# One block kernel: a norm weight spread by products, last steps by banks, two matrices moved to VectorE, later attention turns

## The chip, the cores and the metric

The kernel runs on one core of a Trainium2 chip. The metric is device time in microseconds (us) of one execution; lower is better. The engines are named as in the profile: PE (TensorE products), PEld (TensorE weight loads), DVE (VectorE), ACT (ScalarE), POOL (GpSimd) and SP (the queue that issues nearly all transfers).

## The reference

The input is x of 256 rows by 1024 columns in float32. Two layers follow one another, each of three phases that add to x: a first feed-forward part, a mixer, a second feed-forward part.

```python
def _rms_norm(x, g):
    y = xf * lax.rsqrt(jnp.mean(xf * xf, axis=-1, keepdims=True) + NORM_EPS)
    return (y * g.astype(jnp.float32)).astype(x.dtype)

h = _rms_norm(x, ffn1_norm_pre[l])
x = x + 0.5 * _rms_norm(_swiglu(h, ffn1_w_gate[l], ffn1_w_up[l], ffn1_w_down[l]), ffn1_norm_post[l])
h = _rms_norm(x, mix_norm_pre[l])
x = x + _rms_norm(_mixer(h, w_in[l], ...), mix_norm_post[l])
h = _rms_norm(x, ffn2_norm_pre[l])
x = x + 0.5 * _rms_norm(_swiglu(h, ffn2_w_gate[l], ffn2_w_up[l], ffn2_w_down[l]), ffn2_norm_post[l])
```

The feed-forward width is 2816. The mixer multiplies h by w_in (8520 columns) and feeds three branches: sparse attention with a selected set of 64 keys (job `dsa`), a recurrence over 256 steps in eight heads of 64 (RWKV), and differential attention (job `diff`: two softmaxes, the second one subtracted with a factor lambda, then a norm of each head). Sigmoid gates weigh the three projected branches, their sum goes through w_out.

## The kernel before

Rows of x are held in two tiles of 128 tokens, called t = 0 and t = 1. Every weight is loaded in float32 (`raw`, at most 1 MB in one transfer, two buffers) and split into a rounded part `wh`, cast by ACT, and the rest `wl`, subtracted by DVE; both are of 128x1024. The activations are split in the same way (`hh`, `hl`), and one product becomes three: rest times `wh`, main times `wh`, main times `wl` (`mm3`, lines 229 to 235). Products of 512 columns are issued about 0.23 us apart.

`steps_b` makes a list of steps for one product of a tile: a step has a load and split (`ld`) and the products of one tile t (`go`). For the last product of a phase (w_down in 22 steps, w_out in 8) the output has 1024 columns, two PSUM banks of 512. `run_skew` puts the steps in order: the first `head` steps run for t = 0 and then for t = 1, the middle ones alternate t, and the last `tail` = 7 steps run for t = 0 and then for t = 1, so that tile 0 ends earlier than tile 1 and its norms have the time of tile 1's seven steps. Splits of these seven steps go to seven extra buffers.

`post_norm` (line 384) follows the last step of a tile: two squares with a sum on ACT (L330), the sum and epsilon on DVE (L332), the power of -1/2 on POOL (L333), then for each half a multiplication by the root and the weight from PSUM (L391) and one by the factor with the addition to x (L392). `pre_norm` (line 336) does the same for the norm ahead of the next phase (L330, L332, L333, L353), and its `rest` transposes the result on PE (L362) and splits it into `h`. The place of these transposes in PE's queue is set by `run_skew`: the deferred call is taken ahead of the last step of the other tile.

At the very start the weight of the first norm (`gpre`) is loaded as 128 copies of one row (512 KB). 13 products of zeros run on PE before the norm of tile 0, and 6 behind its transposes (`keep_warm`, L172).

In the mixer, attention and recurrence are generators (`dsa`, `diff`, and one that runs `rwkv_pre`, `rwkv_solve` and `rwkv`). After every step of the gate products, `tick` advances each job by one `yield`, so that their small products stand between the large ones in PE's queue. The order inside an engine is fixed when the program is built, and an engine works through it in order: the first instruction that waits holds up all behind it. In `rwkv_solve` the inverses of 16x16 blocks come back from DRAM as `zs` and `xs`; DVE spreads `zs` over four matrices `Z` (L1032), POOL spreads `xs` over two matrices `T` (L1036), and three levels of products with masks follow (`W`, L1063, and the update of `Z`, L1074). In `diff`, each pair of heads has scores `lm` (L767), a softmax (L653 to L656), two combining operations (L773, L774), then `LAG` = 2 yields, and the transposes of `lm` on PE (L196).

Of the kernel before, what the change touches and what calls it, by code (L numbers as in the profile page):

```python
# [22 lines left out]
WARM = 13, 6  # L23
# [16 lines left out]
class Block:  # L40
    def __init__(self, tc, ins, out, ctx):
# [21 lines left out]
        self.first = ()  # L63
# [39 lines left out]
    def constants(self):  # L103
# [8 lines left out]
        jf = jz[:, :128]  # L112
        with self.pn():
            nc.gpsimd.iota(jf, pattern=[[1, 128]], base=0, channel_multiplier=-1, allow_small_or_imprecise_dtypes=True)
# [98 lines left out]
    def split(self, src, k, n, pool=None):  # L213
# [3 lines left out]
        with self.p0(), self.behind(*(self.first if self.last is None else ())):  # L217
            pair = self.split_to(hi, lo, src)
        if self.last is None:
            self.first = pair  # L220
# [17 lines left out]
    def run_skew(self, steps, head=0, tail=0):  # L238

        n = len(steps)  # L240
        order = [(t, i) for t in range(2) for i in range(head)]
        order += [(t, i) for i in range(head, n - tail) for t in range(2)]
        order += [(t, i) for t in range(2) for i in range(n - tail, n)]
        held = {}
        for j, (t, i) in enumerate(order):
            if self.later and (head and j == head - 1 or tail and j == len(order) - 1):
                self.later.pop(0)()
            if t == 0:
                wait = RING <= i < head or i >= n - tail
                held[i] = steps[i][0](self.extra if wait else self.ring)  # L250
            steps[i][1](t, held[i])
            self.tick()

    def steps_b(self, rows, n, ksteps, xk, psum, done=None):
# [5 lines left out]
        def mk(k0):  # L260
# [7 lines left out]
            def go(t, w):  # L268
# [8 lines left out]
                if k0 + per == ksteps and done is not None:  # L277
# [45 lines left out]
    def rstd(self, parts, width):  # L323
# [8 lines left out]
        nc.vector.tensor_scalar(r, ss[:, 0:1], ss[:, 1:2], EPS, op0=OP.add, op1=OP.add)  # L332
# [3 lines left out]
    def pre_norm(self, t):  # L336
# [11 lines left out]
        with self.pn():  # L348
            xs = [self.x[t][:, h * 512:(h + 1) * 512] for h in range(2)]
            r = self.rstd(xs, D)  # L350
            for h in range(2):
                xn = self.junk.tile([128, 512], F32, name="xn")
                nc.vector.scalar_tensor_tensor(xn, xs[h], r, g[:, h * 512:(h + 1) * 512], op0=OP.mult, op1=OP.mult)  # L353
                xns.append(xn)

        def rest():

            with self.pn(), self.behind(self.last):
# [6 lines left out]
                if self.last is None:  # L365
                    self.first = pair
# [373 lines left out]
    def diff(self, st, vd):  # L740
# [10 lines left out]
        for t in range(2):  # L751
# [5 lines left out]
            for h2 in range(2):  # L757
# [17 lines left out]
                for _ in range(LAG):  # L775
# [24 lines left out]
            yts.append(yt)  # L800
        for _ in range(2 * LAG):
# [194 lines left out]
    def rwkv_solve(self, Ls, strip):  # L996
# [32 lines left out]
        for q in range(4):  # L1029
# [4 lines left out]
            if q < 2:  # L1034
# [234 lines left out]
```

## Time and profile before

| what | value |
|---|---|
| three runs of the kernel | 1435.26 us median (1435.07 to 1437.74) |
| the profiled execution | 1437.46 us, its span 1435.8 us |
| PE busy | 1399.8 us, 97% of the span |
| DVE busy | 1012.3 us, 71% |
| ACT busy | 713.2 us, 50% |
| POOL busy | 77.5 us, 5% |
| mean granted clock of PE | 0.996 |
| read from HBM | 241.80 MB |

The span runs from the first to the last instruction of the profiled execution; its own time is 1.66 us more. A row of the timeline has its start, its length, engine, line, operation, output and inputs, their shapes, and a count where neighbours are merged; in brackets stands how long the engine stood idle before it, and what ended the wait. PE's records overlap: a product of 512 columns is shown with 0.39 us although the next one starts 0.23 us later.

### The profile page before, as it was taken

The numbers are of one execution on the slowest core, as the hardware profiler recorded it, in microseconds if no ns is written. First come the engines' busy times: TensorE is split into PE (matmuls) and PEld (weight loads), VectorE is DVE, ScalarE is ACT, GpSimd is POOL, SyncE is SP. The second block draws the span as 40 slices with busy tenths as digits, with TensorE's granted clock in tenths as the row PEclk, the third lists the DMA queues.
The fourth block names the chain that finished last, engine by engine and source line by source line (L and its number), as shares of the span: only waits on it lengthen the run. The fifth ranks groups of instructions, "written<-read, shape, count | busy, mean of one in ns | idle before, by whom it ended". The sixth has DMA issues, their size and how long they took to land.

```text
span 1435.8 us, 20311 instructions
## 1 busy us (share of the span) xinstructions
PE 1399.8 (97%) x8077; PEld 1203.1 (84%) x8077; DVE 1012.3 (71%) x1496; ACT 713.2 (50%) x1090; POOL 77.5 (5%) x92
## 2 busy tenths in 40 slices
PE   8999999999899999999999999999999999999997
PEld 5888879999688878888888888799887888788886
DVE  5777564988666877776567764659977668768753
ACT  5444454656463554444454444555545635544442
POOL 1000010121100000000000000100300000000000
PEclk9999999999999999999999999999999999999999
DMA  6665665455332564665646656554443326555653
GB/s 220 189 192 194 216 223 186 122 175 152 102 118 89 184 211 148 194 200 200 225 147 189 192 201 237 174 180 147 147 136 101 135 86 226 173 175 178 215 182 114
DMA packets 176407, 246.91 MB, mean 172 GB/s; under 512 B 17908, under 2 KB 128440, under 8 KB 176312
## 3 DMA queue, kind: packets, MB, share of 16 engines
q1 hardware_dynamic: 176312, 245.62, 52.6%
q8 instruction: 63, 1.03, 0.3%
q14 instruction: 32, 0.26, 0.1%
HBM read 241.80 MB, written 3.80 MB: 171 GB/s over the span
## 4 chain that ended last, share of the span: by engine, by line
PE 79%; DVE 9%; DMA 6%; ACT 3%; issue 2%; POOL 0%; SPq 0%; DVEq 0%; POOLq 0%; ACTq 0%
PE ps L310 28%; PE ps L233 11%; PE ps L235 11%; PE ps L234 11%; PE ps L193 7%; DVE wl L224 4%; PE ps L229 3%; PE ps L230 3%; PE ps L231 3%; ACT wh L224 2%; DMA raw<-in_w_in_dram 1%; DMA raw<-in_w_out_dram 1%; PE ps L196 1%; DMA zs<-d 1%; DMA raw<-in_ffn_w_gate_dram 1%
## 5 line engine op out<-in xcount | busy, mean ns | idle before, releaser
L224 DVE TENSOR_TENSOR wl<-raw,wh 128x1024 fp32r<-128x1024 f32 x438 | 531.8, 1222 | 240.4 <-ACT wh L224 239.2
L224 ACT CAST wh<-raw 128x1024 fp32r<-128x1024 f32 x438 | 452.9, 1045 | 453.3 <-PE ps L310 183.4
L310 PE MATMUL ps<-h,wh 128*128 128x512 f32 x1152 | 392.5, 393 | 0.0
L310 PE MATMUL ps<-h,wl 128*128 128x256 f32 x1152 | 300.2, 281 | 0.0
L310 PEld LDWEIGHTS ps<-h,wh 128*128 128x128 f32 x1152 | 206.1, 188 | 37.1
L310 PEld LDWEIGHTS ps<-h,wl 128*128 128x128 f32 x1152 | 216.9, 188 | 12.4
L233 PE MATMUL ps<-wh,h 128*128 128x512 f32 x384 | 160.0, 417 | 2.2 <-DVE h L224 1.9
L229 PE MATMUL ps<-h,wh 128*128 128x256 f32 (+1 forms) x560 | 158.6, 283 | 0.0
L230 PE MATMUL ps<-h,wh 128*128 128x256 f32 (+1 forms) x560 | 156.8, 280 | 0.0
L235 PE MATMUL ps<-wl,h 128*128 128x512 f32 x384 | 153.1, 399 | 2.8 <-DVE wl L224 2.8
L231 PE MATMUL ps<-h,wl 128*128 128x256 f32 (+1 forms) x560 | 155.7, 278 | 0.0
L234 PE MATMUL ps<-wh,h 128*128 128x512 f32 x384 | 152.2, 396 | 0.0
L233 PE MATMUL ps<-wh,gl 128*128 128x512 f32 x352 | 137.3, 390 | 0.0
L235 PE MATMUL ps<-wl,gh 128*128 128x512 f32 x352 | 137.0, 389 | 0.0
L234 PE MATMUL ps<-wh,gh 128*128 128x512 f32 x352 | 136.9, 389 | 0.0
L229 PEld LDWEIGHTS ps<-h,wh 128*128 128x128 f32 (+1 forms) x560 | 104.8, 187 | 2.0 <-issue 1.3
L230 PEld LDWEIGHTS ps<-h,wh 128*128 128x128 f32 (+1 forms) x560 | 104.9, 187 | 0.3
L231 PEld LDWEIGHTS ps<-h,wl 128*128 128x128 f32 (+1 forms) x560 | 104.7, 187 | 0.1
L235 PEld LDWEIGHTS ps<-wl,h 128*128 128x128 f32 x384 | 72.7, 189 | 22.6 <-DVE wl L224 5.6
L233 PEld LDWEIGHTS ps<-wh,h 128*128 128x128 f32 x384 | 72.5, 189 | 20.2 <-issue 3.3
L234 PEld LDWEIGHTS ps<-wh,h 128*128 128x128 f32 x384 | 72.8, 190 | 13.4
L235 PEld LDWEIGHTS ps<-wl,gh 128*128 128x128 f32 x352 | 66.1, 188 | 13.9
(272 smaller groups left out, 1715.0 us busy)
## 6 DMA issues: line engine op xcount, KB each, us to landing
raw<-in_w_in_dram SPq DMA_DIRECT2D x66, 1024.0 KB, 5.1
raw<-in_ffn_w_up_dram SPq DMA_DIRECT2D x44, 1024.0 KB, 5.4
raw<-in_ffn_w_down_dram SPq DMA_DIRECT2D x44, 1024.0 KB, 4.9
raw<-in_ffn_w_gate_dram SPq DMA_DIRECT2D x43, 1024.0 KB, 5.4
raw<-in_w_branch_dram SPq DMA_DIRECT2D x12, 1024.0 KB, 4.9
raw<-in_w_out_dram SPq DMA_DIRECT2D x8, 1024.0 KB, 5.6
gpre<-in_ffn_norm_pre_dram SPq DMA_DIRECT2D x4, 512.0 KB, 5.2
gpost<-in_ffn_norm_post_dram SPq DMA_DIRECT2D x4, 512.0 KB, 6.3
```

What stands on the lines that cost most here:

```text
L193: self.small = self.nc.tensor.matmul(*a, **k)
L196: self.small = self.nc.tensor.transpose(*a, **k)
L224: return self.nc.scalar.copy(hi, src), self.nc.vector.tensor_sub(lo, src, hi.bitcast(F32))
L229: mm(ps, wh, xl, start=first, stop=False)
L230: mm(ps, wh, xh, start=False, stop=False)
L231: self.last = mm(ps, wl, xh, start=False, stop=last)
L233: mm(ps, xl, wh, start=first, stop=False)
L234: mm(ps, xh, wh, start=False, stop=False)
L235: self.last = mm(ps, xh, wl, start=False, stop=last)
L310: self.last = mm(*a, start=k == i == 0, stop=k == 7 and i == 1)
```

## The change

Five edits are made together. (1) The weight of the very first norm is loaded as one row (4 KB) and spread over 128 partitions by two float32 products with a column of ones, into two PSUM banks; the products of zeros become 6, then 4 behind the spreading, then 6; the first splits of weights are ordered anew against the norm. (2) The last seven steps of a phase run by tile and by bank: all seven for bank 0, then all seven for bank 1. (3) In the norms the sum with epsilon goes from DVE to POOL, and in `post_norm` the weight and the factor are multiplied first, the root is applied in the addition to x. (4) The two matrices `T` are made by DVE, behind the third and fourth `Z`. (5) `diff` yields four times in place of two between the softmax and its transposes, and once more at the end of each tile.

```diff
-WARM = 13, 6
+WARM = 6, 4, 6
...
-        order += [(t, i) for t in range(2) for i in range(n - tail, n)]
+        order += [(t, i, b) for t in range(2) for b in range(2) for i in range(n - tail, n)]
...
-            if self.later and (head and j == head - 1 or tail and j == len(order) - 1):
+            if self.later and (head and j == head - 1 or tail and j == len(order) - 2):
...
-                    for b in range(nb):
+                    for b in range(nb) if only is None else (only,):
...
-        nc.vector.tensor_scalar(r, ss[:, 0:1], ss[:, 1:2], EPS, op0=OP.add, op1=OP.add)
+        nc.gpsimd.tensor_scalar(r, ss[:, 0:1], ss[:, 1:2], EPS, op0=OP.add, op1=OP.add)
...
-            self.gpre = self.bcast(self.ins[f"{ph}_norm_pre"][l], D, self.gbp, "gb", "gpre")
+            row = self.ins[f"{ph}_norm_pre"][l]
+            if self.last is None:
+
+                g = self.gbp.tile([128, D], F32, name="grow", tag="gb")[0:1, :]
+                with self.p0():
+                    nc.sync.dma_start(g, bass.AP(tensor=row.tensor, offset=row.offset, ap=[[D, 1], [1, D]]))
+                self.gpre = [self.bank(self.acc) for _ in range(2)]
+                with self.pn():
+                    for h in range(2):
+                        self.tr = nc.tensor.matmul(self.gpre[h], self.ones, g[:, h * 512:h * 512 + 512],
+                                                   start=True, stop=True)
+                self.keep_warm(WARM[1])
...
+            ys = []
             for h in range(2):
+                y = self.junk.tile([128, 512], F32, name="xn")
+                nc.vector.scalar_tensor_tensor(y, ps[h], factor, g[:, h * 512:h * 512 + 512], op0=OP.mult, op1=OP.mult)
+                ys.append(y)
+            for h, y in enumerate(ys):
                 s = slice(h * 512, h * 512 + 512)
-                y = self.junk.tile([128, 512], F32, name="xn")
-                nc.vector.scalar_tensor_tensor(y, ps[h], r, g[:, s], op0=OP.mult, op1=OP.mult)
-                nc.vector.scalar_tensor_tensor(self.x[t][:, s], y, factor, self.x[t][:, s], op0=OP.mult, op1=OP.add)
+                nc.vector.scalar_tensor_tensor(self.x[t][:, s], y, r, self.x[t][:, s], op0=OP.mult, op1=OP.add)
...
-                for _ in range(LAG):
+                for _ in range(2 * LAG):
                     yield
...
             yts.append(yt)
+            yield
...
-            if q < 2:
+            if q > 1:
                 Ts.append(self.ep.tile([128, 4, 128], F32, name="T", tag="s"))
-                nc.gpsimd.tensor_tensor(Ts[q].rearrange("p v (g x) -> p v g x", x=16),
-                                        xs[:, 4 * q:4 * q + 4, None, :].to_broadcast([128, 4, 8, 16]), even, op=OP.mult)
+                nc.vector.tensor_tensor(Ts[-1].rearrange("p v (g x) -> p v g x", x=16),
+                                        xs[:, 4 * q - 8:4 * q - 4, None, :].to_broadcast([128, 4, 8, 16]), even, op=OP.mult)
```

VectorE's queue in the first mixer, from the arrival of `zs` on, before (`blk` is the mask of 16x16 blocks, `lm` the scores of `diff`, `nmd` and `smd` its row maxima and sums, `wl` the rest of a weight split):

```order
L1032 TENSOR_TENSOR Z<-zs,blk_1732 128x512 x3
L224 TENSOR_TENSOR wl<-raw,wh 128x1024
L1032 TENSOR_TENSOR Z<-zs,blk_1732 128x512
L767 SCALAR_TENSOR_TENSOR lm<-ps,cmS 128x256
L224 TENSOR_TENSOR wl<-raw,wh 128x1024
L767 SCALAR_TENSOR_TENSOR lm<-ps,cmS 128x256
L653 TENSOR_REDUCE nmd<-lm 128x4
L1063 TENSOR_TENSOR W<-ps,blk_1732 128x512 x2
L224 TENSOR_TENSOR wl<-raw,wh 128x1024
L656 RECIPROCAL smd<-smd 128x4
L773 TENSOR_SCALAR lm<-lm,smd,lam 128x128 x2
L774 SCALAR_TENSOR_TENSOR lm<-lm,smd 128x128 x2
```

and now:

```order
L1056 TENSOR_TENSOR Z<-zs,blk_1735 128x512 x3
L227 TENSOR_TENSOR wl<-raw,wh 128x1024
L1060 TENSOR_TENSOR T<-xs,even 128x512
L1056 TENSOR_TENSOR Z<-zs,blk_1735 128x512
L227 TENSOR_TENSOR wl<-raw,wh 128x1024
L1060 TENSOR_TENSOR T<-xs,even 128x512
L790 SCALAR_TENSOR_TENSOR lm<-ps,cmS 128x256 x2
L1087 TENSOR_TENSOR W<-ps,blk_1735 128x512
L676 TENSOR_REDUCE nmd<-lm 128x4
L227 TENSOR_TENSOR wl<-raw,wh 128x1024
L1087 TENSOR_TENSOR W<-ps,blk_1735 128x512
L679 RECIPROCAL smd<-smd 128x4
```

The two `T` stand behind the third and the fourth `Z`, and the row maxima `nmd` have moved behind the first `W`.

TensorE's queue a little later in the same mixer, before (L233 to L235 are gate products, `W,T` those of the solve, `ident,lm` the transposes of the attention, `dk,dq` the next scores):

```order
L193 MATMUL ps<-W,T 128x128 x4
L233 MATMUL ps<-wh,h 128x512
L234 MATMUL ps<-wh,h 128x512
L235 MATMUL ps<-wl,h 128x512
L196 MATMUL ps<-ident,lm 128x128
L233 MATMUL ps<-wh,h 128x512
L196 MATMUL ps<-ident,lm 128x128
L234 MATMUL ps<-wh,h 128x512
L235 MATMUL ps<-wl,h 128x512
L193 MATMUL ps<-W,T 128x128 x4
L193 MATMUL ps<-dk,dq 128x128 x4
```

and now, from the last two gate products ahead of the second `W,T` on (`zc` is a part of `Z` for the next level):

```order
L237 MATMUL ps<-wh,h 128x512
L238 MATMUL ps<-wl,h 128x512
L195 MATMUL ps<-W,T 128x128 x4
L236 MATMUL ps<-wh,h 128x512
L237 MATMUL ps<-wh,h 128x512
L238 MATMUL ps<-wl,h 128x512
L236 MATMUL ps<-wh,h 128x512
L237 MATMUL ps<-wh,h 128x512
L238 MATMUL ps<-wl,h 128x512
L198 MATMUL ps<-ident,zc 128x128 x4
L195 MATMUL ps<-Z,up_3011 128x128 x4
L198 MATMUL ps<-ident,lm 128x128 x2
```

The transposes of `lm` stood between the two `W,T`; now they stand behind the first products of the next level.

TensorE's queue in the last seven steps of the very last phase, tile 0, before, at the first two steps (`ps` with two numbers are the two banks, each new number of `wh` is a step):

```order
L233 MATMUL ps_12645<-wh_12899,gl7_11573 128x512
L234 MATMUL ps_12645<-wh_12899,gh7_11562 128x512
L235 MATMUL ps_12645<-wl_12900,gh7_11562 128x512
L233 MATMUL ps_12646<-wh_12899,gl7_11573 128x512
L234 MATMUL ps_12646<-wh_12899,gh7_11562 128x512
L235 MATMUL ps_12646<-wl_12900,gh7_11562 128x512
L233 MATMUL ps_12645<-wh_12911,gl8_11574 128x512
L234 MATMUL ps_12645<-wh_12911,gh8_11563 128x512
L235 MATMUL ps_12645<-wl_12912,gh8_11563 128x512
L233 MATMUL ps_12646<-wh_12911,gl8_11574 128x512
L234 MATMUL ps_12646<-wh_12911,gh8_11563 128x512
L235 MATMUL ps_12646<-wl_12912,gh8_11563 128x512
```

and now, at the sixth and seventh step of bank 0:

```order
L236 MATMUL ps_12648<-wh_12943,gl10_11579 128x512
L237 MATMUL ps_12648<-wh_12943,gh10_11568 128x512
L236 MATMUL ps_12649<-wh_12902,gl7_11576 128x512
L237 MATMUL ps_12649<-wh_12902,gh7_11565 128x512
L238 MATMUL ps_12648<-wl_12944,gh10_11568 128x512
L236 MATMUL ps_12648<-wh_12950,gl10_11579 128x512
L237 MATMUL ps_12648<-wh_12950,gh10_11568 128x512
L238 MATMUL ps_12649<-wl_12903,gh7_11565 128x512
L236 MATMUL ps_12649<-wh_12911,gl8_11577 128x512
L238 MATMUL ps_12648<-wl_12951,gh10_11568 128x512
L237 MATMUL ps_12649<-wh_12911,gh8_11566 128x512
L238 MATMUL ps_12649<-wl_12912,gh8_11566 128x512
```

Each step is now used by three products of one bank and then the next step comes; products of bank 1 with the first splits stand between those of bank 0 that take the last two splits.

## Rows read from the trace of the kernel before

**Rows 1.** The page's head and its busy time of PE: us, share of the span, instructions.

```profile
span 1435.8 us, 20311 instructions
PE 1399.8 (97%) x8077; PEld 1203.1 (84%) x8077; DVE 1012.3 (71%) x1496; ACT 713.2 (50%) x1090; POOL 77.5 (5%) x92
```

**Rows 2.** The waits of PE over the whole span: who waited for whom, us in total, times, the longest.

```profile
PE ps L362 <- DVE xn L353: 5.6, 4, 2.0
PE ps L193 <- DVE Z L1032: 5.0, 5, 1.8
PE ps L196 <- DVE lm L774: 4.1, 2, 2.1
...
PE ps L193 <- DVE W L1063: 1.6, 2, 1.0
PE ps L193 <- DVE yt L798: 1.3, 2, 0.7
```

**Rows 3.** The timeline of the first mixer where `zs` arrives and after it; the last row is the same pair of products one level on.

```profile
362.25 4.04 DVE L1032 TENSOR_TENSOR Z<-zs,blk 128x512 f32<-128x512 f32 x3 [4.67 <-DMA zs<-d]
362.65 3.09 POOL L1036 TENSOR_TENSOR T<-xs,even 128x512 f32<-128x512 f32 x2 [31.59 <-DMA xs<-d]
364.75 0.68 PE L193 MATMUL ps<-Z,up 128*128 128x128 f32 x4 [0.98 <-DVE Z L1032]
367.35 0.68 DVE L1032 TENSOR_TENSOR Z<-zs,blk 128x512 f32<-128x512 f32 x1
...
371.29 1.13 PE L193 MATMUL ps<-W,T 128*128 128x128 f32 x8 [1.04 <-DVE W L1063]
375.17 0.30 PE L196 MATMUL ps<-ident,lm 128*128 128x128 f32 x1 [2.05 <-DVE lm L774]
376.58 1.91 PE L193 MATMUL ps<-W,T 128*128 128x128 f32 x8
386.25 1.05 PE L193 MATMUL ps<-W,T 128*128 128x128 f32 x8
```

**Rows 4.** Busy time by stretches of 10 us (and one of 1 us) in the two mixers: stretch and its length, busy time and instructions of PE, PEld, DVE, ACT, POOL, then the granted clock of PE, the DMA share and GB/s.

```profile
370.00:380.00 10.00, 6.91 (x37) 5.55 (x36) 6.98 (x15) 5.03 (x14) 0.00 (x0) 0.83 0.51 179
376.00:377.00 1.00, 1.00 (x4) 0.81 (x4) 0.00 (x0) 0.90 (x2) 0.00 (x0) 0.50 1.01 369
1070.00:1080.00 10.00, 7.25 (x33) 5.83 (x32) 7.79 (x9) 0.76 (x1) 3.17 (x2) 0.83 0.20 41
1080.00:1090.00 10.00, 7.34 (x38) 5.80 (x37) 6.96 (x15) 5.04 (x14) 0.00 (x0) 0.83 0.50 175
410.00:420.00 10.00, 10.00 (x62) 7.32 (x59) 8.98 (x16) 6.00 (x14) 0.00 (x0) 1.00 0.33 105
```

**Rows 5.** The timeline where a phase ends: the post-norm of tile 0 in the first mixer and the transposes of the next norm; the end of the first feed-forward part of the second layer; the transposes behind the second mixer.

```profile
524.69 0.59 ACT L330 ACTIVATE junk<-ps 128x512 bf16<-128x512 f32 x1
526.25 0.56 POOL L333 TENSOR_TENSOR rstd<-rstd,mhalf 128x1 f32<-128x1 f32 x1 [57.35 <-DVE rstd L332]
526.84 1.41 DVE L391 SCALAR_TENSOR_TENSOR xn<-ps,rstd,gpost 128x512 f32<-128x512 f32 x2 [0.67 <-POOL rstd L333]
532.23 0.63 PE L362 MATMUL ps<-ident,xn 128*128 128x128 f32 x4 [1.84 <-DVE xn L353]
...
900.24 2.00 ACT L224 CAST wh<-raw 128x1024 fp32r<-128x1024 f32 x2 [2.35 <-DMA raw<-in_w_in_dram]
903.78 1.22 DVE L224 TENSOR_TENSOR wl<-raw,wh 128x1024 fp32r<-128x1024 f32 x1
904.01 1.39 POOL L333 TENSOR_TENSOR rstd<-rstd,mhalf 128x1 f32<-128x1 f32 x1 [5.16 <-DVE rstd L332]
906.24 0.99 PE L362 MATMUL ps<-ident,xn 128*128 128x128 f32 x5 [1.96 <-DVE xn L353]
...
1240.99 0.63 PE L362 MATMUL ps<-ident,xn 128*128 128x128 f32 x4 [1.36 <-DVE xn L353]
```

**Rows 6.** The timeline of the last phase: the last two splits of w_down, the first square of tile 0, the same of tile 1, and the last two transfers of the output.

```profile
1412.35 2.36 DVE L224 TENSOR_TENSOR wl<-raw,wh 128x1024 fp32r<-128x1024 f32 x2 [3.16 <-ACT wh L224]
1418.24 0.60 ACT L330 ACTIVATE junk<-ps 128x512 bf16<-128x512 f32 x1 [4.98 <-PE ps L235]
1427.82 0.60 ACT L330 ACTIVATE junk<-ps 128x512 bf16<-128x512 f32 x1 [8.15 <-PE ps L235]
1432.24 0.93 SPq L394 DMA_DIRECT2D out_dram<-xr  x2
```

**Rows 7.** The timeline of the start, and one group of float32 products of 256 columns in the mixer (four records are two products).

```profile
1.26 5.73 PE L172 MATMUL ps<-jf 128*128 128x512 bf16 x13 [1.26 <-DVE jf L110]
6.66 1.44 DVE L353 SCALAR_TENSOR_TENSOR xn<-x,rstd,gpre 128x512 f32<-128x512 f32 x2 [0.54 <-POOL rstd L333]
8.66 1.46 PE L172 MATMUL ps<-jf 128*128 128x512 bf16 x6
10.94 0.63 ACT L330 ACTIVATE junk<-x 128x512 bf16<-128x512 f32 x1 [0.55 <-DMA x<-in_x_dram]
17.26 0.50 PE L235 MATMUL ps<-wl,h 128*128 128x512 f32 x1 [1.68 <-DVE wl L224]
...
393.34 1.13 PE L193 MATMUL ps<-dk,dq 64*128 64x256 f32 x4
```

More of the change, by code (lines that the diff above doesn't have):

```diff
@@ L112, in constants @@
         jf = jz[:, :128]
+        self.ones = jz[0:1, 384:512]
+        nc.vector.memset(self.ones, 1.0)
         with self.pn():
@@ L216, in split @@
         lo = pool.tile([128, 1024], F32R, name="wl", tag="wl")[:, :k * n].rearrange("p (k n) -> p k n", n=n)
-        with self.p0(), self.behind(*(self.first if self.last is None else ())):
+        with self.p0(), self.behind(*self.first):
             pair = self.split_to(hi, lo, src)
         if self.last is None:
-            self.first = pair
+            self.opened = pair
+        self.first, self.firsts = self.firsts, ()
         return hi, lo
@@ L240, in run_skew @@
         n = len(steps)
-        order = [(t, i) for t in range(2) for i in range(head)]
-        order += [(t, i) for i in range(head, n - tail) for t in range(2)]
-        order += [(t, i) for t in range(2) for i in range(n - tail, n)]
+        order = [(t, i, None) for t in range(2) for i in range(head)]
+        order += [(t, i, None) for i in range(head, n - tail) for t in range(2)]
+        order += [(t, i, b) for t in range(2) for b in range(2) for i in range(n - tail, n)]
         held = {}
-        for j, (t, i) in enumerate(order):
-            if self.later and (head and j == head - 1 or tail and j == len(order) - 1):
+        for j, (t, i, b) in enumerate(order):
+            if self.later and (head and j == head - 1 or tail and j == len(order) - 2):
                 self.later.pop(0)()
-            if t == 0:
+            if i not in held:
                 wait = RING <= i < head or i >= n - tail
                 held[i] = steps[i][0](self.extra if wait else self.ring)
-            steps[i][1](t, held[i])
+            steps[i][1](t, held[i], b)
             self.tick()
@@ L276, in go @@
                                  k0 + kk == 0, k0 + kk == ksteps - 1, False)
-                if k0 + per == ksteps and done is not None:
+                if k0 + per == ksteps and done is not None and only in (None, nb - 1):
                     done(t, ps[t])
@@ L342, in pre_norm @@
             ph, l = self.phases[0]
-            self.gpre = self.bcast(self.ins[f"{ph}_norm_pre"][l], D, self.gbp, "gb", "gpre")
+            row = self.ins[f"{ph}_norm_pre"][l]
[9 more added lines that the diff above has]
+                self.keep_warm(WARM[1])
+            else:
+                g = self.bcast(row, D, self.gbp, "gb", "gpre")
+                self.gpre = [g[:, h * 512:h * 512 + 512] for h in range(2)]
             self.new_h()
@@ L352, in pre_norm @@
                 xn = self.junk.tile([128, 512], F32, name="xn")
-                nc.vector.scalar_tensor_tensor(xn, xs[h], r, g[:, h * 512:(h + 1) * 512], op0=OP.mult, op1=OP.mult)
+                i = nc.vector.scalar_tensor_tensor(xn, xs[h], r, g[h], op0=OP.mult, op1=OP.mult)
                 xns.append(xn)
+            if self.last is None:
+                self.first = (i,)
         def rest():
@@ L365, in rest @@
                 if self.last is None:
-                    self.first = pair
+                    self.firsts = pair
         if self.last is None:
@@ L1220, in second @@
         def second():
-            with b.behind(*b.first):
+            with b.behind(*b.opened):
                 b.pre_norm(1)
@@ L1227, in hybrid_block @@
         b.pre_norm(0)
-        b.keep_warm(WARM[1])
+        b.keep_warm(WARM[2])
         b.after_load = lambda: load_x(1)
```

4 lines of the change are left out of this document (2 added, 2 removed).

## The prediction

> **What bounds the kernel now.** I read the page's head first. PE is busy for 1399.8 of 1435.8 us [rows 1], and no edit takes a large product away, so at most some 36 us are in reach, and only where PE stands still or runs slowly. The second view is PE's waits: five kinds hold most of the idle time in the middle of the run, 5.6, 5.0, 4.1, 1.6 and 1.3 us [rows 2]. Each lies beside one of the edits: transposes of a normed tile (L362), the first products of the recurrence's solve (Z, W), the transposes of attention scores (lm), a bank held by yt. The third view is the timeline there. The matrices Z should take 0.68 us each, as the last one does, but three take 4.04 us while POOL makes T for 3.09 us [rows 3]. Then PE stands still for 2.05 us at the transposes of lm, and the pair W,T behind it takes 1.91 us, where the same pair a level later takes 1.05 [rows 3]. The fourth view says why: the granted clock is 0.50 there, the lower level (1.2 GHz), after a stretch of idle time; over 10 us it is 0.83, and in the second layer two stretches have 0.83 [rows 4]. Each costs (1 - 0.83) x 10 = 1.7 us of PE's work. So a wait in the mixer costs more than its length.
>
> **The start.** The chain is: tile 0 arrives, norm, transposes, split, first product. The weight's transfer falls from 512 KB to 4 KB. Ahead of the landing of tile 1 (10.9 us [rows 7]) lay five pieces of 512 KB; an estimate by a fifth of the some 9.5 us in which they moved lets tile 1 come 1.9 us earlier. PE waits 1.68 us for the third split of weights at 17.26 [rows 7]. VectorE's work from the end of tile 0's norm (6.66 + 1.44 = 8.10 [rows 7]) to that split is three splits (3 x 1.22 [rows 5]), two halves of tile 1's norm (1.4, as for tile 0 [rows 7]) and two splits of h with small constants, some 2.2: together 7.3. It could be ready at 15.4 instead of 17.2, 1.8 earlier. Against it stand the two spreading products. Two float32 products of 256 columns take 1.13 us [rows 7], so one of 512 takes about 1.1 at full speed. PE is not at full speed there: 13 products of zeros take 5.73 us, 0.44 each, the later six 1.46, 0.24 each [rows 7]. At half speed the two take up to 4.5 us and end near 8.3, about 0.9 later than VectorE wants the second half, and four products of zeros follow ahead of the transposes. I take +1.2 us, between a gain of 3 (the wait and the earlier tile in full) and a loss of 1.5 (the first product late by that much, nothing regained).
>
> **The last steps and the norms.** Three waits at L362 count: 1.84, 1.96 and 1.36 us [rows 5]; the fourth of the 5.6 us is at the start. By banks, the first bank's square (0.59 [rows 5], with its read-out about 0.75) and both multiplications from PSUM (1.41 [rows 5]) leave the chain between a tile's last product and its next norm; the sum on POOL adds what DVE's sum and the hand-over took, or a little more. That is some 2.1 us shorter. At the first and third place I take 1.1 and 1.3 of the 1.84 and 1.36, since ACT still casts two splits ahead of the second square. At the second place the norm's squares stand behind two casts that wait for a transfer until 900.24 [rows 5]; that stays, and I take 0.6 of the 1.96. Sum 3.0.
>
> The price is in the splits. One bank uses a split in three products (3 x 0.23 = 0.69 us), and VectorE makes one in 1.22 [rows 5]. In the last phase bank 0's square starts at 1418.24 [rows 6], bank 1 ends three products later, so the seven steps began at 1418.92 - 42 x 0.23 = 1409.3. The sixth split is needed as the fifth product of the sixth step's stretch, at 1409.3 + 19 x 0.23 = 1413.7, and is ready at 1413.5; the seventh is needed at 1414.8 and ready at 1412.35 + 2.36 = 1414.7 [rows 6]. The products of bank 1 that stand in between just cover it; without them it would be late by up to 0.9. I take -0.4 for the four feed-forward phases, bounds 0 and -4 x 0.9. The end of the kernel: from tile 1's first square (1427.82) to its last output (1432.24 and its second issue [rows 6]) one square (0.7) and one pair of multiplications (1.41 [rows 5]) go, but the first bank's square already began ahead of the last products and the sum on POOL costs about 0.2 more; +1.2, bounds 0.7 and 2.1. Together +3.8, bounds -1 and 6.5.
>
> A sum of POOL beside a split is the weak point: the power takes 0.56 us alone, and 1.39 when a split of 1.22 runs on VectorE [rows 5]. The Trainium skill (GPSIMD Engine Reference, 1. Specifications) says that POOL shares its SBUF interfaces with VectorE and contends with instructions that have two SBUF inputs; the trace agrees. By that rule the moved sum would be held too, which speaks against the edit; it is the third rival.
>
> **T on VectorE.** Now the first three Z end after 3 x 0.68 = 2.04 us in place of 4.04, and ahead of the last Z a split and one T follow. It ends at 362.25 + 2.04 + 1.22 + 0.68 + 0.68 = 366.9 instead of 367.35 + 0.68 = 368.0, 1.1 earlier. The second T (0.68) stands ahead of the first W, but the row maxima have gone behind it, which are of like length. So W and the pair W,T come 1.1 earlier, in either layer: +2.2, bounds 0.5 (if T takes POOL's 1.55 on VectorE) and 4 (the Z and W waits of 6.6 us [rows 2], less what the arrival of zs sets).
>
> **The attention turns.** The two waits for lm (4.1 us) and for yt (1.3 us) [rows 2] go, as the transposes stand nine large products later, in the next level. The lower clock behind the lm wait goes in both layers: 2 x 1.7 = 3.4. Gross 8.8. What is late next: the next level's zc waits for the update of Z, which VectorE does behind the softmax; I count 0.45 per layer. The rows of the second tile's softmax go from 410 us, where VectorE is busy for 8.98 of 10 us [rows 4], into the recurrence's second half. No row shows that mixture; bounds are 0 and VectorE's own work for one such softmax, some 4.3 us, at two places in either layer. I take 1.5 per layer, nearest to the first mixer's other waits (0.98 and 1.04 [rows 3]). Net 8.8 - 0.9 - 3.0 = +4.9.
>
> **Sum.** 1.2 + 3.8 + 2.2 + 4.9 = 12.1 us. The profiled execution would go from 1437.46 to 1425.4. It lies 2.2 above the median of the three runs, 1435.26; against that the forecast is 1423.2, say 1423.
>
> **Rivals.** *All waits go and none comes back.* The new waits of 3.9 do not appear, the first low clock of the second layer (1.7) goes too, the start gives 1.5 more: 12.1 + 7.1 = 19.2, 1416. For it: the order leaves large products between all small ones. Against it: VectorE is busy beside them.
>
> *The mixer gives its gain back.* W takes the place of lm as what PE waits for, and the clock falls all the same: the 4.9 are lost, and 1 of T. 6.2 us remain, 1429. For it: W is waited for already with 1.04 us.
>
> *POOL is held behind splits.* The moved sum takes 1.39 like the power: 0.83 more, for two norms at the three places, 5.0: 12.1 - 5.0 = 7.1, 1428. Against it: VectorE's queue now has the norm's own work at those moments, so no split runs beside it.
>
> *The start and the banks cost what they give.* The spreading products end late (-1.5 instead of +1.2), the splits are late in all phases (-3.6 instead of -0.4), and the mixer's new waits are 2 larger in each layer: 12.1 - 2.7 - 3.2 - 4 = 2.2, 1433, no change that can be told.
>
> *Slower.* The second tile's softmax stands in VectorE's queue ahead of the masks and the state that the second half of the recurrence needs. PE waits for all of it, 4.3 us at two places in either layer, and the clock falls for 1.7 more in each: 2 x (8.6 + 1.7) = 20.6 against 12.1 + 3.0 = 15.1 without my allowance: 5.5 slower, 1441. It decides from 7.5 us of waits in a layer. For it: VectorE's 8.98 of 10 us. Against it: PE has shown no wait there so far, and much of the softmax falls into a stretch between two products' results.
>
> That the edits do not do what they say is not among them: the order shows the transposes, T and the banks moved.
>
> **Chances.** Forecast 0.50, everything gained 0.16, mixer gives back 0.15, POOL held 0.08, nothing in sum 0.07, slower 0.04. About 0.2%, 2.9 us, is what a measurement can tell from no change, so faster begins below 1432.4: 0.50 + 0.16 + 0.15 + 0.08 = 0.89, less 0.01 for the upper edge of the giving back, 0.88; within 0.2% 0.08; slower 0.04. The range goes from 1414, with most of the full gain in, to 1431, with the two middle rivals in; it leaves out some 0.18.
>
> **What would show it.** Right: three Z in about 2 us with no POOL beside them; no wait for lm above 0.5 us; a granted clock of 1.00 where 370 to 380 and 1080 to 1090 had 0.83; L362 waits near 0.7, 1.3 and 0.1 us; no wait of PE for wl in the last seven steps above 0.3 us; tile 1's first square near 9 us. Wrong: a wait for W, S or lk of over 1 us in the recurrence, a first large product later than 12 us, or sums on POOL of over 1 us.

## The result and the profile after

The changed kernel takes 1425.07 us (median of 4 executions, 1423.06 to 1426.78). The kernel before, run beside it, takes 1436.5 (1435.07 to 1440.2). The ratio is 0.9921, its 95% interval 0.9896 to 0.9945: faster, by 11.4 us of medians (0.8%). The profiled execution of after took 1423.06 us (span 1421.4), against 1437.46.

The page's head and its busy times, as in [rows 1]:

```profile
span 1421.4 us, 20365 instructions
PE 1398.2 (98%) x8078; PEld 1200.5 (84%) x8078; DVE 1006.8 (71%) x1477; ACT 713.2 (50%) x1090; POOL 83.4 (6%) x112
```

PE is busy for nearly as long (1398.2 us against 1399.8); of the 14.4 us by which the span is shorter, 12.8 are time in which PE stood still, and 1.6 are busy time, in which its slower stretches count too. The waits of PE after, to be held against [rows 2] (L1056 is Z, L1087 W, L382 the transposes of the normed tile, L238 the product with `wl`):

```profile
PE ps L195 <- DVE Z L1056: 2.4, 3, 1.7
PE ps L236 <- DVE h L227: 1.9, 2, 1.0
...
PE ps L238 <- DVE wl L227: 1.7, 1, 1.7
PE ps L195 <- DVE yc L1203: 1.6, 2, 0.8
...
PE ps L195 <- DVE lk L1145: 1.1, 2, 0.5
PE ps L195 <- DVE W L1087: 0.8, 1, 0.8
PE ps L382 <- DVE xn L371: 0.8, 1, 0.8
```

The waits for lm and yt are gone, those for xn fell from 5.6 to 0.8, Z from 5.0 to 2.4. New are yc and lk, which stand in the recurrence's second half; the wait for `ml`, the rest of a split activation, grew from 0.5 to 1.3. The timeline of after, in order of time: the start, the first product of the first mixer, its solve and its end, the first product of the second mixer, Z and the end of that mixer, and the end of the kernel:

```profile
4.30 3.75 PE L356 MATMUL ps<-grow,jf 1*128 1x512 f32 x4 [0.32 <-DMA grow<-in_ffn_norm_pre_dram]
7.98 1.89 PE L174 MATMUL ps<-jf 128*128 128x512 bf16 x4
8.09 0.75 DVE L371 SCALAR_TENSOR_TENSOR xn<-x,rstd,ps 128x512 f32<-128x512 f32 x1 [0.52 <-PE ps L356]
9.66 1.91 PE L382 MATMUL ps<-ident,xn 128*128 128x128 f32 x8
12.97 0.58 PE L236 MATMUL ps<-wh,h 128*128 128x512 f32 x1
18.46 0.50 PE L238 MATMUL ps<-wl,h 128*128 128x512 f32 x1 [1.73 <-DVE wl L227]
19.50 1.04 PE L382 MATMUL ps<-ident,xn 128*128 128x128 f32 x8
...
212.55 0.50 PE L236 MATMUL ps<-wh,h 128*128 128x512 f32 x1 [0.96 <-DVE h L227]
...
363.26 1.90 DVE L1056 TENSOR_TENSOR Z<-zs,blk 128x512 f32<-128x512 f32 x3 [4.68 <-DMA zs<-d]
366.20 0.69 DVE L1060 TENSOR_TENSOR T<-xs,even 128x512 f32<-128x512 f32 x1
370.55 1.16 PE L195 MATMUL ps<-W,T 128*128 128x128 f32 x8 [0.83 <-DVE W L1087]
376.60 0.38 PE L198 MATMUL ps<-ident,lm 128*128 128x128 f32 x2
...
520.86 0.94 POOL L336 TENSOR_SCALAR rstd<-ss 128x1 f32<-128x1 f32 x1 [56.29 <-ACT junk L334]
524.89 0.30 POOL L336 TENSOR_SCALAR rstd<-ss 128x1 f32<-128x1 f32 x1 [2.45 <-ACT junk L334]
526.78 1.29 PE L382 MATMUL ps<-ident,xn 128*128 128x128 f32 x8
...
913.21 0.51 PE L236 MATMUL ps<-wh,h 128*128 128x512 f32 x1 [0.96 <-DVE h L227]
...
1065.61 1.29 PE L195 MATMUL ps<-Z,up 128*128 128x128 f32 x8 [1.72 <-DVE Z L1056]
...
1221.32 0.93 POOL L336 TENSOR_SCALAR rstd<-ss 128x1 f32<-128x1 f32 x1 [55.29 <-ACT junk L334]
1227.51 1.29 PE L382 MATMUL ps<-ident,xn 128*128 128x128 f32 x8 [0.76 <-DVE xn L371]
...
1414.77 0.39 PE L238 MATMUL ps<-wl,gh 128*128 128x512 f32 x1
1415.26 0.60 ACT L334 ACTIVATE junk<-ps 128x512 bf16<-128x512 f32 x1 [4.05 <-PE ps L238]
```

Three Z take 1.90 us where they took 4.04 [rows 3], the transposes of lm and of the normed tile (376.60, 526.78) show no wait; those at 1227.51 wait 0.76 us. The start is later: tile 1's transposes begin at 19.50, in place of 18.29. The same work in the kernel before: the first large product, tile 1's transposes, the first products of the two mixers, and the last product:

```profile
10.44 0.50 PE L233 MATMUL ps<-wh,h 128*128 128x512 f32 x1 [0.33 <-ACT wh L224]
18.29 1.03 PE L362 MATMUL ps<-ident,xn 128*128 128x128 f32 x8
...
211.43 0.51 PE L233 MATMUL ps<-wh,h 128*128 128x512 f32 x1 [0.95 <-DVE h L224]
...
920.41 0.51 PE L233 MATMUL ps<-wh,h 128*128 128x512 f32 x1 [0.90 <-DVE h L224]
...
1428.02 0.39 PE L235 MATMUL ps<-wl,gh 128*128 128x512 f32 x1
```

The granted clock by stretches (columns as in [rows 4]):

```profile
370.00:380.00 10.00, 9.45 (x66) 8.33 (x68) 7.95 (x16) 7.26 (x19) 0.00 (x0) 1.00 0.40 130
1065.00:1070.00 5.00, 4.39 (x19) 3.80 (x20) 5.00 (x7) 1.05 (x1) 0.00 (x0) 0.71 0.20 33
1080.00:1090.00 10.00, 10.00 (x69) 8.82 (x68) 7.60 (x16) 6.15 (x17) 0.00 (x0) 1.00 0.34 107
```

Of the three stretches at the lower level one is left, behind the wait of 1.72 us for Z (stretches behind the last product, where PE has nothing to do, are not counted here or below). Where the 14.4 us came from can be read by setting the two timelines against each other at work that both do: at the first product of the first mixer (212.55 after, 211.43 before) the new kernel is 1.1 us behind; at the first product of the second mixer (913.21 and 920.41) 7.2 ahead; at the last product (1414.77 and 1428.02) 13.25 ahead; and from there to the end of the span 6.6 against 7.8 us give the last 1.2.

### The profile page after: what moved, and what is told of

It reads as the page before. It is cut to its first block, busy times and chain, and to the rows that moved or that the text cites. A ratio compares the mean times of both kernels' runs of the same rounds, so it can differ in the third digit from the quotient of the medians.

```text
span 1421.4 us, 20365 instructions
## 1 busy us (share of the span) xinstructions
PE 1398.2 (98%) x8078; PEld 1200.5 (84%) x8078; DVE 1006.8 (71%) x1477; ACT 713.2 (50%) x1090; POOL 83.4 (6%) x112
## 5 line engine op out<-in xcount | busy, mean ns | idle before, releaser
L233 PE MATMUL ps<-h,wh 128*128 128x256 f32 (+1 forms) x560 | 157.0, 280 | 0.0
L238 PE MATMUL ps<-wl,h 128*128 128x512 f32 x384 | 152.1, 397 | 1.7 <-DVE wl L227 1.7
L238 PE MATMUL ps<-wl,gh 128*128 128x512 f32 x352 | 137.5, 391 | 0.1
L233 PEld LDWEIGHTS ps<-h,wh 128*128 128x128 f32 (+1 forms) x560 | 105.0, 188 | 0.3
L238 PEld LDWEIGHTS ps<-wl,h 128*128 128x128 f32 x384 | 72.3, 188 | 19.4 <-DVE wl L227 3.0
L238 PEld LDWEIGHTS ps<-wl,gh 128*128 128x128 f32 x352 | 66.1, 188 | 15.6 <-DVE wl L227 1.5
```

What stands on the lines that cost most here:

```text
L233: mm(ps, wh, xh, start=False, stop=False)
L238: self.last = mm(ps, xh, wl, start=False, stop=last)
```

## The experiments

Each kernel was timed beside the kernel before; the table gives its median and the ratio to before. The lines below it tell what was changed.

| kernel | median us | ratio (95% interval) | mean granted clock, executions |
|---|---|---|---|
| before, beside three sets of these | 1435.0 to 1436.5 | 1 | 0.9946, 54 |
| changed | 1425.07 | 0.9921 (0.9896 to 0.9945) | 0.9972, 4 |
| before + T on VectorE | 1431.16 | 0.9959 (0.9943 to 0.9976) | 0.9970, 12 |
| before + attention turns | 1430.67 | 0.9960 (0.9946 to 0.9974) | 0.9968, 12 |
| changed, T on POOL | 1426.80 | 0.9938 (0.9921 to 0.9955) | 0.9973, 6 |
| changed, old turns | 1427.99 | 0.9943 (0.9923 to 0.9963) | 0.9978, 8 |
| changed, both mixer edits undone | 1434.95 | 0.9983 (0.9969 to 0.9997) | 0.9942, 12 |
| changed, last steps in old order | 1424.87 | 0.9925 (0.9899 to 0.9950) | 0.9975, 6 |
| changed, edits 2 and 3 undone | 1427.80 | 0.9947 (0.9929 to 0.9966) | 0.9963, 7 |
| changed, old start | 1423.09 | 0.9911 (0.9882 to 0.9939) | 0.9978, 4 |
| changed, no zeros behind the spreading | 1421.76 | 0.9904 (0.9876 to 0.9932) | 0.9985, 4 |
| changed, third split first | 1421.39 | 0.9906 (0.9873 to 0.9939) | 0.9982, 4 |
| no zeros and third split first | 1420.58 | 0.9887 (0.9870 to 0.9904) | 0.9980, 4 |
| old start and third split first | 1420.29 | 0.9881 (0.9865 to 0.9898) | 0.9988, 4 |

**The clock in this table.** Executions of one kernel differ, and most of the difference goes with the clock: with each kernel's own mean taken out, the 141 executions scatter about a line of 1.2 us for each 0.001 of mean granted clock (correlation -0.78, so six tenths of the variance). Of the kernel before, one execution took 1431.66 us at 0.999 and another 1443.68 at 0.990. It is a correlation: a longer wait of PE could lower the clock and lengthen the execution at once. A profile of one execution, or a median of four, is uncertain by some us, and kernels are best compared with their mean clocks beside them; the medians of the kernel before differ by 1.6 us from set to set, so kernels of different sets are better compared by their ratios.

### The mixer: T and the attention turns

T alone in the kernel before:

```diff
-            if q < 2:
+            if q > 1:
...
-                nc.gpsimd.tensor_tensor(Ts[q].rearrange(...
+                nc.vector.tensor_tensor(Ts[-1].rearrange(...
```

> The kernel before with the two matrices T on VectorE alone; nothing else changed. Theory of separate gains: three Z take 2.0 us in place of 4.04, the first W comes about 1.1 us earlier in either layer, the lm wait of 2.05 us stays, the kernel is some 2.2 us faster (bounds 0.5 and 4). Rival, one chain: the transposes of lm wait for VectorE's softmax, which stands behind the same T, so lm waits longer (2.5 us or more) for what Z and W give, and the kernel is within 0.7 us of before.

It is 4.2 us faster by medians than the kernel before beside it (1435.41), 5.9 by the ratio. VectorE's Z and the transposes of lm in that run:

```profile
363.12 1.90 DVE L1032 TENSOR_TENSOR Z<-zs,blk 128x512 f32<-128x512 f32 x3 [4.61 <-DMA zs<-d]
373.90 0.30 PE L196 MATMUL ps<-ident,lm 128*128 128x128 f32 x1 [1.63 <-DVE lm L774]
```

The Z are as expected. The wait for lm got shorter (1.63, was 2.05), not longer, so the one-chain rival falls; and no stretch at the lower clock follows it here. The mean clock is 0.0022 above that of the kernel before beside it, by the line above 2.6 us, which the 2.2 us expected had left out.

The attention turns alone in the kernel before:

```diff
-                for _ in range(LAG):
+                for _ in range(2 * LAG):
...
             yts.append(yt)
+            yield
```

> The kernel before with the later attention turns alone; T stays on POOL. Separate gains: the lm and yt waits (2.05 and 0.66 per layer) go, the stretches of lower clock behind lm go, 0.45 us for zc and up to 1.5 us of new waits per layer come; 5 us faster (3 to 8). Rival, the waits only wander: PE waits for Z, W or zc by over 1.5 us more per layer, a granted clock of 0.50 shows all the same, and the kernel is at most 2 us faster.

4.7 us faster by medians (5.7 by the ratio): the separate gain, near the 5. Waits for lm and yt are gone, yc (0.78) and lk (0.54) have come in both layers.

The same two edits taken out of the changed kernel, one at a time (the diffs above turned round):

> The changed kernel with T back on POOL. Separate gains: three Z take about 4 us again, waits for Z of about 1 us per layer return, 2.2 us slower than the changed kernel (1427.3). Rival, the gain of 9.8 us that the two mixers show together needs both edits: the lower clock returns in both layers behind the Z waits, and it is 5 us or more slower (1430).

> The changed kernel with the attention turns as before; T stays on VectorE. Separate gains: lm waits of about 2 us and yt waits of 0.66 us return in both layers, with a stretch of granted clock 0.50 behind each lm wait; 5 to 7.6 us slower than the changed kernel (1430 to 1432.5). Rival, T on VectorE already frees the softmax: lm waits stay under 1 us and it is at most 2.5 us slower (1427.5).

1.7 and 2.9 us slower by medians, 2.4 and 3.2 by the ratios. For T that is the separate gain: three Z take 4.04 us again, PE's waits for Z go from 2.4 to 5.0, and no lower clock shows in the mixers. With the old turns the waits for lm (1.63 and 1.62 us) and yt (0.66) are back, but the cost is less than the 5 expected; in the profile the clock stayed up behind both waits for lm, and fell behind both for yt (397 to 401 and 1100 to 1104). Two edits that are worth 4.2 and 4.7 when they come first and 1.7 and 2.9 when they come last have something in common. Both taken out:

> The changed kernel with both mixer edits undone (T on POOL, attention turns as before). Each alone, put into the kernel before, gave 4.2 and 4.7 us by medians; each alone, taken out of the changed one, cost 1.7 and 2.9. Theory of overlap: both remove the same wait for VectorE's softmax and the low clock behind it, so the two together are worth less than the sum of 8.9: 5 to 7.5 us, 1430 to 1432.5. Rival, separate gains: 1433.5 or more. Second rival, the mixer is worth only the 4.6 of the two takings out: 1429.7 or less.

1434.95: 9.9 us slower than the changed kernel by medians, 8.9 by the ratios. The medians look like separate gains (4.2 + 4.7 = 8.9), but they don't agree among themselves: one edit put in and then the other should make the whole, and they give 4.2 + 2.9 = 7.1 and 4.7 + 1.7 = 6.4. The ratios do agree: 5.9 + 3.2 = 9.1 and 5.7 + 2.4 = 8.1, beside 8.9. By them the two gains put in alone make 11.6, and 2.7 of it are counted twice: the edits overlap, though the 5 to 7.5 us expected for both were too few. What the two share shows in the clock column of the table. Without either edit the mean granted clock is 0.9942 (0.9946 in the kernel before); with either of them, or with both, it is 0.997 to 0.998. Stretches of 2 us of the kernel with both edits undone, and its waits of PE in the mixers:

```profile
376.00:378.00 2.00, 2.00 (x10) 1.89 (x8) 0.64 (x2) 1.95 (x4) 0.00 (x0) 0.50 1.00 377
398.00:400.00 2.00, 2.00 (x9) 1.63 (x8) 0.50 (x2) 1.07 (x2) 0.00 (x0) 0.56 0.00 0
1076.00:1078.00 2.00, 2.00 (x7) 1.58 (x6) 2.00 (x3) 0.00 (x0) 0.00 (x0) 0.50 0.00 0
1086.00:1088.00 2.00, 2.00 (x9) 1.81 (x9) 0.59 (x2) 1.95 (x4) 0.00 (x0) 0.50 1.00 383
```

```profile
PE ps L195 <- DVE Z L1055: 4.5, 5, 1.3
PE ps L198 <- DVE lm L797: 4.1, 2, 2.1
...
PE ps L195 <- DVE W L1086: 1.7, 2, 1.0
PE ps L195 <- DVE yt L821: 1.3, 2, 0.7
```

These are four of its five stretches at the lower level, behind waits for lm, yt and Z; the changed kernel's profile has one. At 1.2 us for each 0.001, 0.9972 - 0.9942 = 0.0030 is 3.6 us of the 9.9; 6.3 are waits. With T undone the clock stays (0.9973) and 1.7 us are waits alone; with the turns undone it is 0.0006 higher, so 2.9 + 0.7 = 3.6 are waits. 1.7 + 3.6 = 5.3 of 6.3: the waits about add up, and the clock is what either edit brings back. By the ratios it is 8.9 - 3.6 = 5.3 of waits for both, against 2.4 + 3.9 = 6.3 taken out one at a time and 3.3 + 3.3 = 6.6 put in. The intervals reach 2 to 3.5 us to either side, and the 0.0006 is within the scatter of four and eight executions, so the overlap and its split are a reading, not a measurement.

### The norms and the last steps

```diff
-        order += [(t, i, b) for t in range(2) for b in range(2) for i in range(n - tail, n)]
+        order += [(t, i, None) for t in range(2) for i in range(n - tail, n)]
...
-            if self.later and (head and j == head - 1 or tail and j == len(order) - 2):
+            if self.later and (head and j == head - 1 or tail and j == len(order) - 1):
```

> The changed kernel with the last seven steps in the old order (both banks in each step, deferred transposes ahead of the last step). Theory: the banks carry most of the 4.3 us that the trace shows at the three waits for the normed tile: waits of 1.2 us or more return at two of the three, the end of the kernel is 0.7 us later, in all 2.5 to 4 us slower (1428 to 1429). Rival: the banks give at most what their splits cost, and the gain there is from the order inside the norm and the sum on POOL: within 1 us of the changed kernel (1425).

1424.87, no difference that can be told (the interval is 3.6 us to either side); the rival's number. Waits for xn of 0.98 and 1.15 us are back at two places, and five short waits for `wl` of 0.15 to 0.35 us, where the next phase begins, just ahead of tile 1's transposes. In waits that is 2.1 + 1.2 - 0.8 = 2.5 us of one profile, which the times don't confirm. Nor can the waits for xn be put to the banks: kernels that have them and differ from the changed one at the start alone show as much at the same two places, 0.94 and 0.56 us with the third split first, 1.53 and 0.46 without the zeros as well. The end of the kernel, from the last product to the end of the span, is as short as in the changed kernel (1427.2 - 1420.51 = 6.7 us against 6.6). Then edit 3 undone as well:

```diff
-        nc.gpsimd.tensor_scalar(r, ss[:, 0:1], ss[:, 1:2], EPS, op0=OP.add, op1=OP.add)
+        nc.vector.tensor_scalar(r, ss[:, 0:1], ss[:, 1:2], EPS, op0=OP.add, op1=OP.add)
...
-                nc.vector.scalar_tensor_tensor(y, ps[h], factor, g[:, h * 512:h * 512 + 512], op0=OP.mult, op1=OP.mult)
...
-                nc.vector.scalar_tensor_tensor(self.x[t][:, s], y, r, self.x[t][:, s], op0=OP.mult, op1=OP.add)
+                nc.vector.scalar_tensor_tensor(y, ps[h], r, g[:, s], op0=OP.mult, op1=OP.mult)
+                nc.vector.scalar_tensor_tensor(self.x[t][:, s], y, factor, self.x[t][:, s], op0=OP.mult, op1=OP.add)
```

> The changed kernel with the whole of edits 2 and 3 undone: the last seven steps by step, the sum with epsilon on VectorE, post_norm with root and weight first. With the old order of steps alone the median was 1424.87. Theory: the order inside post_norm carries the gain at the three waits for the normed tile: they are back near 1.8, 2.0 and 1.4 us, the end is 1 us later, and the time is 1429 to 1430. Rival: edits 2 and 3 are hardly worth anything, the waits are back but other waits fall by as much, 1426 or less.

2.7 us slower than the changed kernel by medians, 3.7 by the ratios; its fastest of seven executions (1427.3) is slower than the slowest of the four (1426.78). By the line above 1.1 us of it go with the clock. PE's waits for xn in it, and its last product:

```profile
PE ps L382 <- DVE xn L371: 3.1, 3, 1.3
```

```profile
1418.35 0.39 PE L238 MATMUL ps<-wl,gh 128*128 128x512 f32 x1
```

Three waits are back (1.33, 0.80, 0.94), smaller than in the kernel before and not far above those just named, and the end takes 1426.1 - 1418.35 = 7.75 us, 1.1 more. So it lies between the two expectations, and the 1.1 us at the end belong to edit 3, not to the banks. No run parts the two halves of edit 3, the sum on POOL and the order inside `post_norm`, or undoes it with the banks kept.

### The start

```diff
-            if self.last is None:
...
+            g = self.bcast(row, D, self.gbp, "gb", "gpre")
+            self.gpre = [g[:, h * 512:h * 512 + 512] for h in range(2)]
...
-WARM = 6, 4, 6
+WARM = 13, 6
```

> The changed kernel with the start of the kernel before: the weight of the first norm as 128 copies (512 KB), 13 and 6 products of zeros, the old order of the first splits. Theory: the new start costs what the trace shows, tile 1's transposes start 1.2 us earlier (18.3 in place of 19.50) and the kernel takes 1423.9 us. Rival: the loss is taken up by later waits (the wait for sq at 300 us), and the time stays within 0.5 us of the changed kernel.

2.0 us faster by medians, 1.4 by the ratios, with intervals that overlap. Tile 1's transposes begin at 18.02 (19.50 in the changed kernel), and the first mixer's first product at 211.03 (212.55), 1.5 us earlier. That the new start is late there does not rest on one profile: the four profiles with the old start have that product at 211.03 to 211.43 (the old start with the third split first is not among them), the six with the new start unchanged at 212.18 to 213.31. What of it arrives at the end is less so. In this profile the lead is gone by the first mixer's `zs` (Z at 365.41, in place of 363.26), behind a longer wait for sq, with the clock at 0.50 from 302 to 306:

```profile
300.81 0.58 PE L195 MATMUL ps<-bones,sq 128*128 128x2 f32 x2 [2.16 <-ACT sq L902]
```

That wait is 1.21 us in the changed kernel and 0.71 to 2.48 in the other profiles, without a plain relation to the start, so the rival is neither shown nor excluded; the median is on the theory's side. What in it:

```diff
-WARM = 6, 4, 6
+WARM = 6, 0, 6
```

> The changed kernel without the four products of zeros behind the two spreading products. Theory one: these 1.9 us hold up the transposes; they start near 8.9 in place of 9.66, the first large product near 12.0 in place of 12.97, and tile 1's transposes come up to 1 us earlier. Theory two: the two spreading products (3.75 us at half speed) are the loss, and the zeros are what bring PE to full speed: without them transposes and zeros run at half speed until later and tile 1's transposes stay at 19.5 or come later.

Its timeline:

```profile
4.00 3.75 PE L356 MATMUL ps<-grow,jf 1*128 1x512 f32 x4
7.67 2.03 PE L382 MATMUL ps<-ident,xn 128*128 128x128 f32 x8
9.49 2.77 PE L174 MATMUL ps<-jf 128*128 128x512 bf16 x6
11.70 0.99 PE L236 MATMUL ps<-wh,h 128*128 128x512 f32 x1
16.59 0.50 PE L238 MATMUL ps<-wl,h 128*128 128x512 f32 x1 [0.78 <-DVE wl L227]
17.64 1.04 PE L382 MATMUL ps<-ident,xn 128*128 128x128 f32 x8
```

The transposes start 2.0 us earlier (7.67), tile 1's 1.9 earlier, and the median is 3.3 lower (1.6 of it by the clock, 0.0013 higher). Theory two is half right: PE does stay slow for longer (six products of zeros take 2.77 us, 1.46 in the kernel before [rows 7]), but that costs less than the zeros did. Then the order at the third split (`b.rest` is the last split made):

```diff
-                i = nc.vector.scalar_tensor_tensor(xn, xs[h], r, g[h], op0=OP.mult, op1=OP.mult)
+                with self.behind(self.third):
+                    i = nc.vector.scalar_tensor_tensor(xn, xs[h], r, g[h], op0=OP.mult, op1=OP.mult)
...
+                b.third = b.rest
                 b.pre_norm(1)
+                b.third = None
```

> The changed kernel with one order turned: the two multiplications of tile 1's first norm stand behind the third split of weights on VectorE, not ahead of it. Theory: PE's wait of 1.73 us for that split at 18.46 is VectorE's queue and falls below 0.4, tile 1's transposes start 1.2 us earlier (18.3). Rival: the wait moves to the transposes, which then wait 1 us or more for xn, and nothing is gained.

The wait for the third split is gone and no wait for xn has come at tile 1's transposes; these begin at 17.90 in place of 19.50, the first mixer's first product at 211.40 in place of 212.55. The wait was VectorE's order. The median is 3.7 us lower, of which 1.15 are seen there and 1.2 go with the clock (0.0010 higher). The two together:

> The changed kernel without the four products of zeros and with tile 1's first norm behind the third split. Theory: tile 1's transposes started at 17.64 without the zeros, still behind a wait of 0.78 for the third split; that goes, they start at 16.9 to 17.2 and the kernel takes 1421 us (3.5 to 4 faster than the changed kernel). Rival: the wait moves to the transposes, and it is not faster than either edit alone (1421.4 to 1421.8).

Tile 1's transposes start at 16.75, the first mixer's first product at 209.85, 2.7 us before the changed kernel's. And the old start with the same order:

> The changed kernel with the start of the kernel before and with tile 1's first norm behind the third split. Theory: the wait of 1.74 us for the third split at 16.98 goes, tile 1's transposes start at 16.4 to 16.9 in place of 18.02, and the kernel takes 1421.7 us or less. Rival: they wait for xn by over 1 us, and the time stays at 1423.

```profile
15.54 0.50 PE L239 MATMUL ps<-wl,h 128*128 128x512 f32 x1 [0.30 <-DVE wl L228]
16.58 1.03 PE L370 MATMUL ps<-ident,xn 128*128 128x128 f32 x8
```

The wait for the third split falls from 1.74 to 0.30 us, the first mixer's first product comes at 210.10, and the time of 1420.29 is the lowest of all, though not to be told from the 1420.58 of the one above. Both are faster than the kernel before by 1.1 to 1.2% and than the changed kernel by 4.5 and 4.8 us of medians, of which 2.7 and 2.45 are seen at the first mixer's first product and 1.0 and 1.9 go with the clock. With both mended, the spread row and the 512 KB transfer come to the same: the small transfer buys nothing here that can be told.

## Why the prediction was right, and where it was not

The forecast of 1423 is 2 us from the median of 1425.07. That closeness is in part luck: the start was forecast some 3 us too well and the mixer 2 to 3 too poorly, and the two errors cancel. By terms:

**The start, +1.2: wrong.** It lost: 1.1 us by the timelines, 1.5 at the same product by the old start put back, 1.4 to 2.0 in its time. The failed step is "I take +1.2 us", and in it the third split "ready at 15.4 instead of 17.2". I had summed VectorE's work as if it ran through from 8.10. It does not: the second half of xn waits for the spreading products until 8.09, the transposes stand behind four products of zeros until 9.66 and then take 1.91 us, the first large product starts at 12.97 in place of 10.44, and tile 1's norm still stands ahead of the third split, so PE waits 1.73 us there all the same. Between its two halves of xn and the third split VectorE stood idle for 3.3 us in all, which the sum of 7.3 had left out; 15.4 + 3.3 = 18.7, and the split's product starts at 18.46. The parts were in the text (3.75 us of spreading against "up to 4.5", the zeros "ahead of the transposes"); I took them as the lower bound, -1.5, where they were the chain. An earlier landing of tile 1 can't be read off: its first square stands behind the late casts of h, at 12.09, and without the zeros at 10.22 behind the same cast, not near 9.

**The last steps and norms, +3.8: right as a sum (2.7 to 3.7), wrong as to the banks.** The waits I expected to be left, 0.7, 1.3 and 0.1, were 0, 0 and 0.76: the sum of 4.4 gained in the profile, where I took 3.0, is partly due to where the places fell, since the undoing brought back 3.07 and not 5.16. The waits for `wl` in the last seven steps add up to 0.1 us in the whole kernel, so the price of the banks (-0.4) was none. The end gives 1.2, as forecast, but by edit 3, where I had counted the first bank's square too. For the banks alone no gain could be told.

**T, +2.2, and the turns, +4.9: 7.1 where undoing both measures 9.9 (8.9 by the ratios).** Three Z in 1.90 us, lm and yt gone, the clock of 370 to 380 and 1080 to 1090 at 1.00: as forecast. The clock gave, by the line above, 3.6 us against the 3.4 that I took, but I put it all to the turns, "2 x 1.7", where T alone brings it back too. The waits were undersized. With both edits undone PE waits for Z, lm, yt and W 4.5 + 4.1 + 1.3 + 1.7 = 11.6 us; in the changed kernel for Z, yc, lk and W 2.4 + 1.6 + 1.1 + 0.8 = 5.9. The difference of 5.7 stands against 2.2 + 5.4 - 3.9 = 3.7 of mine. The new waits of 1.5 per layer came at 0.78 + 0.54 = 1.3, for yc and lk; those of 0.9 for zc did not come at all (at 375.27 and 378.21 its transposes show none); and Z and W gave 3.0 in place of 2.2: the first pair W,T starts 7.3 us behind the first Z (370.55 - 363.26), where it took 9.0 [rows 3], 1.75 earlier in place of 1.1.

**The rivals.** "Everything gained" (1416) failed at the start, and because new waits of 1.3 us in a layer and a stretch at the lower clock in the second layer came. "The mixer gives back" did not happen: W is waited for once with 0.83 us. "POOL is held": it is, but the path hardly feels it. The sum takes 0.30 us in 13 of 24 norms and 0.71 to 1.76 in the other eleven, such as 0.94 beside a split of weights on VectorE (520.86 above). The Trainium skill (GPSIMD Engine Reference, 1. Specifications) says the two share SBUF interfaces, and the trace agrees with 0.94 against 0.30. The power, which took up to 1.46 in the kernel before, now takes 0.56 or 0.57 in every norm, so the hold has moved from one to the other. At the three places one sum each is held (0.94, 1.40, 0.93); the transposes behind the first two show no wait, those behind the third 0.76 us, of which at most 0.25, VectorE's wait for POOL there, can be put to it. My sign for this rival, sums over 1 us, came and was badly chosen: it was to be read at PE. My sign of a first large product later than 12 us came as well, at 12.97, and stood rightly for the start. "The start and the banks cost what they give" was right for the start alone. "Slower" needed 7.5 us of waits in a layer, and 1.3 came.

The sum by undoing: start -2.0, norms +2.7, mixer +9.9, together 10.6, against 11.4 of medians; by the ratios -1.4, +3.7 and +8.9, together 11.2 of 11.3.

## What to carry to other kernels

When a late operand is replaced by work on the engine that is waiting (spreading a row by products), count that work and its warming as links of the chain, and then look at what stands ahead of the next wait in the other queue: turning one order on VectorE gave 1.15 us at the first mixer, nearly the 1.5 of putting the old start back. Where PE's clock falls behind short waits, one of several edits may bring it back and the rest then look worthless, or each looks doubly good alone; undo them one by one and all together before a gain is put to one of them. Read the mean granted clock beside every time, since here most of the spread between executions of one kernel goes with it, and compare kernels of different sets by their ratios to a common one, since the medians here did not agree among themselves.

## What was not expected of the hardware

The low stretches do not follow a wait's length in any simple way: behind a wait of 1.63 us for lm the clock stayed up in one kernel, behind 1.72 for Z it fell in another, and with T on POOL three waits of 0.43, 0.98 and 0.89 us in a row left it up. What decides it stays open. At the start the records show the column at 1.00 from the first microsecond, yet six products of zeros take 1.46 us at 8.66 in the kernel before, 2.77 at 9.49 behind the spreading products, which read one row: PE reaches its full pace some 4 us later there, and the clock column doesn't show it.
